# Layer A of a two-layer encoder trunk: two seven-product blocks for each pair of units, and their place in the second unit

## The chip, the cores and the metric

The kernel runs on one core of a Trainium2 chip. The metric is the device time of one execution in microseconds. A core has five engines that run side by side, each through its own instructions in a fixed order: TensorE (PE in the profile; PEld is its loading of the stationary operand), VectorE (DVE), ScalarE (ACT), GpSimd (POOL) and SyncE (SP). They wait for one another by semaphores. Transfers (DMA) are issued from the queues of SP, ACT and POOL. Matmuls write to eight banks of PSUM, a small memory from which DVE and ACT read the results.

## The reference

The input is one sequence of 256 frames of width 2048. There are two layers. Layer A (chunked attention with a relative bias) and layer B (attention with forget gates against shared keys and values) each have 32 heads of 128. What matters here is the first half of layer A:

```python
h = rms_norm(x, a_norm[layer])
q, k, v, g = jnp.split(h @ a_w_in[layer], 4, axis=-1)
o = chunked_relbias_attention(split_heads(q), split_heads(k), split_heads(v),
                              a_rel_bias[layer]).reshape(b, s, D_INNER)
x = x + (o * jax.nn.silu(g)) @ a_w_out[layer]
```

`a_w_in` is 2048 x 16384, `a_w_out` 4096 x 2048, all in float32.

## The kernel before

**Units and blocks.** All projections are cut into *units* of 512 output columns, 256 frames and the whole inner dimension. A unit accumulates in two PSUM banks, one for each half (`t`) of the frames. The inner dimension of layer A's input projection is 2048, that is 16 slices of 128; two slices (KB = 2) are a *block*, so a unit has eight blocks. A block's weights come in one load of 512 KB on SP's queue (`Feed.load`, line 208; six buffers, RAW).

**Splits.** Each float32 factor is split in a high and a low half in the format that TensorE takes at full rate. For a block of weights ACT rounds the high half (line 249 in `Feed.prepare`) and DVE subtracts to get the low half (line 250). A product is then three matmuls: high by high, high by low, low by high (`mm3`, line 178, for plain blocks; `dot3`, line 547, elsewhere). A plain block is 2 slices x 2 halves of the frames x 3 = 12 matmuls. The splits have four buffers each (SPLIT = 4) and are prepared three ahead of the block at which TensorE is (DEPTH = 3, `Feed.fill`). A buffer can be written again when TensorE has read what was in it.

**Groups, pairs and quads.** Two heads (HG = 2) are a group, and there are 16 groups. In layer A a group needs two units, which make a *pair*: one of queries and keys (`aqk`), one of values and gates (`avg`). Where the same block of both units is taken together, there are two slices of x by two halves of the frames on one side, and two slices of weights by two units on the other: a 2 x 2 by 2 x 2 product of tiles. Class `Quad` does it with seven products instead of eight, by the scheme of Strassen in Winograd's form: 21 matmuls instead of 24. It works in four parts (`Quad.split(i)`, i = 0 to 3, one split buffer each; the third is half as wide): the first unit's weights; the sums `t` of the two units' weights (lines 303 and 304); the second unit's second slice; and a last sum, formed in place by lines 312 and 313 on DVE. `Quad.step` (line 316) issues the matmuls, of which some go to the units' own accumulators and four (p1, p5, p7, p6) to four banks of their own. At the last quad of a run ACT and DVE (lines 352 to 356) combine these four into `comb`, which is added when the units are closed. The sums of x that a quad needs are formed once (`Quads.sum_up`, line 387).

Before the change, every pair of layer A from group 1 on has one quad, of block 7, behind the fifth of the seven plain blocks of its first unit (QUAD_STEP = 5). The 14 other blocks are plain.

**Attention beside the matmuls.** The attention of a group is a generator (`side_a`, line 711, and `attention`, line 552) whose steps are carried out between the blocks of the following units. `drive` (line 749) calls `advance` behind the blocks that a table names: `{3: 1}` means one step behind block 3. The steps in order: queries and keys from the accumulators (line 725) to `qk`; their transposition; their splits (`wide`, `q`, line 540 and 541); scores and softmax in two steps; the gates times the softmax's scale (`sg`) and their transposition; the split of the transposed weights; the second product; the output `oT` and its splits. In before, the queries and keys of a group are closed at the start of its second unit, and its attention runs from there into the next pair's second unit.

**Transposition.** `turn` (line 513) transposes 32 x 32 squares on DVE (line 518) and then moves them by 16 small transfers (line 521). In layer A twelve of the 16 of queries and keys are issued by POOL and four by ACT, and all 16 of `sg` by POOL. In layer B POOL and SP issue eight each.

Program order on an engine is the order in which the code issues, moved a little by the layer that builds the program. `issue_after` holds an instruction behind a named one, and `feed.behind` (line 264) is a tiny ACT operation that does the same through data.

## Time and profile before

| | us |
|---|---|
| median of 3 runs | 1731.91 (1731.39 to 1732.01) |
| the profiled execution | 1731.21 |
| its span, first to last instruction | 1729.5 |
| layer A's pairs of groups 1 to 14 (53.82 to 656.18) | 602.36, or 43.03 each |

In the profile a row of a timeline is: start, duration, engine, line, operation, output<-inputs, shape, and in brackets how long the engine had been idle and what ended it. Names of tiles lack their buffer numbers. `first` is the tile that holds the quads' sums `t` in one half and the transposed rows of queries and keys in the other; `sums` holds the sums of x in one half and the transposed queries and keys in the other. A row of windows gives the stretch, its length, and the busy time of each engine with the number of instructions.

### The profile page before, as it was taken

The numbers are of one execution on the slowest core, as the hardware profiler recorded it, in microseconds if no ns is written. First come the engines' busy times: TensorE is split into PE (matmuls) and PEld (weight loads), VectorE is DVE, ScalarE is ACT, GpSimd is POOL, SyncE is SP. The second block draws the span as 40 slices with busy tenths as digits, with TensorE's granted clock in tenths as the row PEclk, the third lists the DMA queues.
The fourth block names the chain that finished last, engine by engine and source line by source line (L and its number), as shares of the span: only waits on it lengthen the run. The fifth ranks groups of instructions, "written<-read, shape, count | busy, mean of one in ns | idle before, by whom it ended". The sixth has DMA issues, their size and how long they took to land.

```text
span 1729.5 us, 26618 instructions
## 1 busy us (share of the span) xinstructions
PE 1714.6 (99%) x8258; PEld 1505.1 (87%) x8258; DVE 1499.0 (87%) x2282; ACT 1186.5 (69%) x2163; POOL 394.7 (23%) x815
## 2 busy tenths in 40 slices
PE   9999999999999999999999999999999999999997
PEld 7888888888888888888888888888888888888886
DVE  7888888888888888888978999999999999996887
ACT  7666666666666666655658787788778887875554
POOL 2332333333333333212102222222222222221000
PEclk9999999999999999999999999999999999999999
DMA  8776777777777767576766666666666666767654
GB/s 307 243 230 226 232 231 230 228 229 229 229 228 226 233 224 233 190 260 216 264 214 222 219 238 230 225 230 231 227 228 233 231 227 228 261 228 247 219 195 146
DMA packets 147245, 396.41 MB, mean 229 GB/s; under 512 B 31104, under 2 KB 45728, under 8 KB 146976
## 3 DMA queue, kind: packets, MB, share of 16 engines
q1 hardware_dynamic: 119248, 363.71, 62.2%
q0 software_dynamic: 24064, 27.84, 5.4%
q10 hardware_dynamic: 3792, 3.17, 0.6%
q8 instruction: 66, 1.08, 0.3%
q14 instruction: 75, 0.61, 0.1%
HBM read 351.05 MB, written 4.23 MB: 205 GB/s over the span
## 4 chain that ended last, share of the span: by engine, by line
PE 96%; DVE 1%; DMA 1%; ACT 1%; issue 0%; SPq 0%; POOL 0%; ACTq 0%; DVEq 0%
PE bkv_acc L186 17%; PE avg_acc L186 17%; PE bqg_acc L186 17%; PE aqk_acc L186 16%; PE bo_acc L186 8%; PE ao_acc L186 7%; PE p L549 2%; PE p L548 2%; PE p L550 2%; PE op L612 1%; PE s0p L572 1%; DMA bo_raw<-in_b_w_out 0%; PE s1p L550 0%; PE s1p L549 0%; PE s1p L548 0%; PE op L550 0%
## 5 line engine op out<-in xcount | busy, mean ns | idle before, releaser
L521 POOL DMA_DIRECT2D sums<-first x320 | 157.3, 499 | 432.8 <-issue 157.8
L521 POOL DMA_DIRECT2D sgZ<-sgY x384 | 188.1, 497 | 154.5 <-DVE sgY L518 96.0
L244 ACT ACTIVATE bqg_hi<-bqg_raw,gain 128x512 fp32r<-128x512 f32 x226 | 150.0, 713 | 85.6 <-DMA bqg_raw<-in_b_w_in 27.4
L245 DVE SCALAR_TENSOR_TENSOR bkv_lo<-bkv_raw,gain,bkv_hi 128x512 fp32r<-128x512 f32 x226 | 162.0, 764 | 18.2 <-ACT bkv_hi L244 17.8
L186 PE MATMUL aqk_acc<-aqk_hi,xTh 128*128 128x512 f32 x452 | 167.5, 382 | 1.0 <-ACT aqk_hi L249 1.0
L249 ACT ACTIVATE avg_hi<-avg_raw 128x1024 fp32r<-128x1024 f32 x112 | 116.1, 1050 | 75.5 <-PE avg_acc L186 49.9
L186 PE MATMUL bkv_acc<-bkv_hi,x1Th 128*128 128x512 f32 x452 | 167.5, 382 | 0.0
L186 PE MATMUL bqg_acc<-bqg_hi,x1Th 128*128 128x512 f32 x452 | 167.4, 382 | 0.0
L186 PE MATMUL avg_acc<-avg_hi,xTh 128*128 128x512 f32 x452 | 167.4, 382 | 0.0
L186 PE MATMUL aqk_acc<-aqk_lo,xTh 128*128 128x512 f32 x452 | 166.3, 379 | 0.7 <-DVE aqk_lo L250 0.7
L186 PE MATMUL bqg_acc<-bqg_hi,x1Tl 128*128 128x512 f32 x452 | 166.1, 379 | 0.0
L186 PE MATMUL avg_acc<-avg_hi,xTl 128*128 128x512 f32 x452 | 166.1, 379 | 0.0
L186 PE MATMUL bqg_acc<-bqg_lo,x1Th 128*128 128x512 f32 x452 | 166.1, 379 | 0.0
L186 PE MATMUL bkv_acc<-bkv_hi,x1Tl 128*128 128x512 f32 x452 | 166.1, 379 | 0.0
L186 PE MATMUL bkv_acc<-bkv_lo,x1Th 128*128 128x512 f32 x452 | 166.1, 379 | 0.0
L186 PE MATMUL aqk_acc<-aqk_hi,xTl 128*128 128x512 f32 x452 | 166.1, 379 | 0.0
L186 PE MATMUL avg_acc<-avg_lo,xTh 128*128 128x512 f32 x452 | 166.1, 379 | 0.0
L250 DVE TENSOR_TENSOR avg_lo<-avg_raw,avg_hi 128x1024 fp32r<-128x1024 f32 x112 | 136.4, 1218 | 31.1 <-ACT avg_hi L249 31.1
L244 ACT ACTIVATE bkv_hi<-bkv_raw,gain 128x512 fp32r<-128x512 f32 x226 | 145.1, 711 | 23.2 <-issue 15.8
L245 DVE SCALAR_TENSOR_TENSOR bqg_lo<-bqg_raw,gain,bqg_hi 128x512 fp32r<-128x512 f32 x226 | 156.3, 742 | 4.8 <-ACT bqg_hi L244 4.8
L250 DVE TENSOR_TENSOR aqk_lo<-aqk_raw,aqk_hi 128x1024 fp32r<-128x1024 f32 x110 | 134.1, 1222 | 25.4 <-ACT aqk_hi L249 17.6
L249 ACT ACTIVATE aqk_hi<-aqk_raw 128x1024 fp32r<-128x1024 f32 x110 | 115.6, 1051 | 42.2 <-PE avg_acc L186 28.5
(379 smaller groups left out, 4332.9 us busy)
## 6 DMA issues: line engine op xcount, KB each, us to landing
bqg_raw<-in_b_w_in SPq DMA_DIRECT2D x128, 512.0 KB, 4.9
bkv_raw<-in_kv_w SPq DMA_DIRECT2D x128, 512.0 KB, 4.8
avg_raw<-in_a_w_in SPq DMA_DIRECT2D x127, 512.0 KB, 4.8
aqk_raw<-in_a_w_in SPq DMA_DIRECT2D x125, 512.0 KB, 4.6
ao_raw<-in_a_w_out SPq DMA_DIRECT2D x64, 512.0 KB, 4.5
bo_raw<-in_b_w_out SPq DMA_DIRECT2D x64, 512.0 KB, 4.4
sgZ<-sgY POOLq DMA_DIRECT2D x384, 40.0 KB, 2.9
sums<-first POOLq DMA_DIRECT2D x320, 32.0 KB, 3.4
```

Source lines behind the costliest of these rows:

```text
L186: pe.matmul(acc[t], x[:, t * P:(t + 1) * P], w, start=t not in begun, stop=last and i == 2)
L244: self.by_act = act.activation(hi[:, j], raw[:, j], AF.Copy, scale=gk)
L245: self.by_dve = dve.scalar_tensor_tensor(lo[:, j], raw[:, j], gk, r32(hi[:, j]), op0=OP.mult, op1=OP.subtract)
L249: self.by_act = act.activation(hi[:, j], raw[:, j], AF.Copy)
L250: self.by_dve = dve.tensor_sub(lo[:, j], raw[:, j], r32(hi[:, j]))
L521: queues[j].dma_start(out=r32(z)[j * SQ:(j + 1) * SQ, i], in_=y[i * SQ:(i + 1) * SQ, j])
L548: pe.matmul(out_, a[0], b[0], start=start, stop=False)
L549: pe.matmul(out_, a[0], b[1], start=False, stop=False)
L550: pe.matmul(out_, a[1], b[0], start=False, stop=stop)
L572: pe.matmul(s0p[:, i], q0[:, i], qkT[:, HG + i, 0], start=True, stop=True)
L612: pe.matmul(op[:, i, 1::NT], v1[:, i * DH:(i + 1) * DH], pT[:, i, NT], start=False, stop=i == HG - 1)
```

## The change

Every pair of layer A from group 1 on gets two quads, of blocks 6 and 7, and twelve plain blocks. They stand in the second unit, behind its plain blocks 1 and 2, so that one plain block lies between them. The first unit's six plain blocks all come before, and its accumulators are complete only at the end of the second quad. There `products` combines, closes queries and keys and issues two steps of the new group's attention (`advance(side, 2)`: `qk`, and its transposition). The remaining steps follow the tables A1_STEPS and A2_STEPS in the next pair. In group 0 the sums of x for both blocks are formed inside the second unit. The transfers of layer A's transpositions are issued by POOL and SP in turn (HALVES), as in layer B, and none by ACT. At the start of the output projection of layer A the last group's steps stand at other places. `feed.behind` in the quads' splits goes, and all quads are held by `issue_after`. Layer B is written differently in a few places but issues what it did.

```diff
-QUAD_STEP = 5
-QUAD_STEP_B = 3
-SECOND_STEPS = {0: 1, 6: 1}
-FIRST_STEPS = {0: 2, 2: 1}
-OLD_A_STEPS = {1: 1, 3: 99}
+QUADS_A = (1, 2)
+QUADS_B = (2,)
+A1_STEPS = {3: 1, 4: 2}
+A2_STEPS = {0: 1, 3: 1, 4: 99}
...
             if not i:
-                if not self.w:
-                    feed.behind(t[:, 0, :, :1], -1)
...
-                with tc.issue_after(feed.by_dve.ins) if self.w else nullcontext():
+                with tc.issue_after(feed.by_dve.ins):
                     dve.tensor_sub(t[:, 0], two[:, 0], one[:, 0])
                     dve.tensor_sub(t[:, 1], two[:, 1], two[:, 0])
...
-    def paired(specs, n):
-
-        quad = Quad(a_quads, specs, KD // KB - 1, True, True)
-        plain = whole(specs[0]) + whole(specs[1])
-        todo.extend(plain[:n] + [(None, quad)] + plain[n:])
-        return quad
-
-    a_pairs = [paired(qkvg[2 * g:2 * g + 2], QUAD_STEP) for g in range(1, NG)]
+    def paired(specs, places):
+
+        n = len(places)
+        quads = [Quad(a_quads, specs, KD // KB - n + i, not i, i == n - 1) for i in range(n)]
+        todo.extend(whole(specs[0]))
+        for i, item in enumerate(whole(specs[1])):
+            todo.append(item)
+            todo.extend((None, quads[k]) for k in range(n) if places[k] == i)
+        return quads
+
+    a_pairs = [paired(qkvg[2 * g:2 * g + 2], QUADS_A) for g in range(1, NG)]
...
+    HALVES = (pool, sp) * (NQ // 2)
...
-        yield from attention(g, biases, qk, vg, halfA, oA, (pool, pool, pool, act), (2, 2), home)
+        yield from attention(g, biases, qk, vg, halfA, oA, HALVES, ("last", "last"), home)
...
+    sums2 = big_tile([P, 2, 2, 4, P], F32R, name="sums2")
     rs, prev = [], None
     for g in range(NG):
         accs = {}
         if g:
             first, second = (Unit(xT, next(order)) for _ in range(2))
-
-            def products():
-                a_pairs[g - 1].step(xT, first, second)
-                for t in range(NT):
-                    act.activation(a_quads.comb[:, t], a_quads.comb[:, t], AF.Copy, scale=rsA[:, t:t + 1])
-
-            accs["qk"] = drive(rest(first), prev, FIRST_STEPS, {QUAD_STEP - 1: products})
-            vg = rest(second)
+            accs["qk"] = drive(rest(first), prev, A1_STEPS)
+            side = side_a(g, accs)
+
+            def products(quad):
+                quad.step(xT, first, second)
+                if quad.last:
+                    for t in range(NT):
+                        act.activation(a_quads.comb[:, t], a_quads.comb[:, t], AF.Copy, scale=rsA[:, t:t + 1])
+                    advance(side, 2)
+
+            hooks = {i: lambda quad=quad: products(quad) for i, quad in zip(QUADS_A, a_pairs[g - 1])}
+            accs["vg"] = list(drive(rest(second), prev, A2_STEPS, hooks))
         else:
             first, second = woven_units()
             rsA, halfA = rs
-            accs["qk"], vg = first.acc, rest(second)
-        old, prev = prev, side_a(g, accs)
-        advance(prev)
-        accs["vg"] = list(drive(vg, prev, SECOND_STEPS, {}, old, OLD_A_STEPS))
-        if not g:
-            a_quads.sum_up(xT, KD // KB - 1, sums[:, 0], a_quads.comb)
+            accs["qk"] = first.acc
+            side = side_a(g, accs)
+            advance(side)
+            sum_hooks = {1: lambda: advance(side)}
+            for i, b in ((2, KD // KB - 1), (4, KD // KB - 2)):
+                sum_hooks[i] = lambda b=b: a_quads.sum_up(xT, b, (sums if b % 2 else sums2)[:, 0], a_quads.comb)
+            accs["vg"] = list(drive(rest(second), None, {}, sum_hooks))
+        prev = side
         close_vg(accs, g)
...
-    project(oA, ao, ao_order, ao_begun, ao_closed, [(prev, [1, 0, 2, 6, 2, 1]), (ao_quads.open(oA, QUADS), [3, 1, 1, 2, 26])])
+    project(oA, ao, ao_order, ao_begun, ao_closed, [(prev, [4, 1, 0, 1, 4, 1, 1]), (ao_quads.open(oA, QUADS), [3, 1, 1, 2, 26])])
```

The built programs show where things stand. First DVE around the quad of a pair before the change (group 3); `sg`, `csc` and `sgY` belong to the attention of the group before:

```order
L250 TENSOR_TENSOR aqk_lo_1490<-aqk_raw_1317,aqk_hi_1489 128x1024
L303 TENSOR_TENSOR first_102<-avg_raw_1337,aqk_raw_1335 128x512
L594 RECIPROCAL csc<-sm 128x4
L595 TENSOR_TENSOR csc<-csc,half_a 128x4
L310 TENSOR_TENSOR quad_lo_1511<-aqk_raw_1335,quad_hi_1510 128x1024
L518 STREAM_TRANSPOSE sgY<-sg 128x1280
L312 TENSOR_TENSOR aqk_raw_1335<-avg_raw_1337,first_102 128x512
L310 TENSOR_TENSOR quad_lo_1555<-first_102,quad_hi_1554 128x1024
L313 TENSOR_TENSOR aqk_raw_1335<-aqk_raw_1335 128x512
L310 TENSOR_TENSOR quad_lo_1571<-avg_raw_1337,quad_hi_1570 128x512
L310 TENSOR_TENSOR quad_lo_1593<-aqk_raw_1335,quad_hi_1592 128x1024
L250 TENSOR_TENSOR aqk_lo_1605<-aqk_raw_1385,aqk_hi_1604 128x1024
```

The same engine in the changed program, from the last low half of the first quad of group 3 to that of the second:

```order
L306 TENSOR_TENSOR quad_lo_1659<-aqk_raw_1419,quad_hi_1658 128x1024
L249 TENSOR_TENSOR avg_lo_1671<-avg_raw_1472,avg_hi_1670 128x1024
L299 TENSOR_TENSOR first_102<-avg_raw_1492,aqk_raw_1490 128x512
L300 TENSOR_TENSOR first_102<-avg_raw_1492 128x512
L306 TENSOR_TENSOR quad_lo_1685<-aqk_raw_1490,quad_hi_1684 128x1024
L306 TENSOR_TENSOR quad_lo_1694<-first_102,quad_hi_1693 128x1024
L308 TENSOR_TENSOR aqk_raw_1490<-avg_raw_1492,first_102 128x512
L306 TENSOR_TENSOR quad_lo_1704<-avg_raw_1492,quad_hi_1703 128x512
L309 TENSOR_TENSOR aqk_raw_1490<-aqk_raw_1490 128x512
L306 TENSOR_TENSOR quad_lo_1722<-aqk_raw_1490,quad_hi_1721 128x1024
```

Before, plain blocks stood on both sides of the one quad; now the second quad's sums and splits stand behind a single plain low half (`avg_lo`). The same lines of code have lower numbers in the changed file: 249 is 250 of before, 299, 300, 308 and 309 are 303, 304, 312 and 313, and 306 is 310.

TensorE at the last part of such a second quad (group 4 of the changed program), with the plain block behind it:

```order
L551 MATMUL avg_acc_1887<-quad_hi_2140,sums 128x512
L549 MATMUL aqk_acc_1886<-quad_hi_2158,xTh_106 128x512
L549 MATMUL p_2094<-quad_hi_2158,sums 128x512
L550 MATMUL aqk_acc_1886<-quad_lo_2159,xTh_106 128x512
L551 MATMUL aqk_acc_1886<-quad_hi_2158,xTl_108 128x512
L550 MATMUL p_2094<-quad_lo_2159,sums 128x512
L551 MATMUL p_2094<-quad_hi_2158,sums 128x512
L185 MATMUL avg_acc_1887<-avg_hi_2170,xTh_105 128x512
```

In the code the three matmuls of each product stand together; in the built order both that need only the high half (`quad_hi`) stand ahead of the first that needs the low half (`quad_lo`). At the first quad of a pair, and everywhere before the change, they stand as in the code.

More of the change, by code (lines that the diff above doesn't have):

```diff
@@ L286, in __init__ @@
             self.all, self.specs, self.b, self.first, self.last = all_, specs, b, first, last
-            self.w = specs[0]["g0"] is not None or all_.w
         def split(self, i):
@@ L358, in trunk, with __init__ @@
     class Quads:
-        def __init__(self, name, w):
-            self.name, self.w, self.sums = name, w, {}
+        def __init__(self, name):
+            self.name, self.sums = name, {}
         def order(self, first, second, n, lead):
@@ L433, in trunk @@
     for g in range(NG):
-        qkvg.append(spec(f"bqg{g}", b_w_in[g], KD, g0=GB, quads=g > 0))
-        qkvg.append(spec(f"bkv{g}", kv_w[g], KD, g0=GKV, quads=g > 0))
+        qkvg.append(spec(f"bqg{g}", b_w_in[g], KD, g0=GB, quads=len(QUADS_B) * (g > 0)))
+        qkvg.append(spec(f"bkv{g}", kv_w[g], KD, g0=GKV, quads=len(QUADS_B) * (g > 0)))
     bo = [spec(f"bo{u}", b_w_out[u], KI, LATE if u == 3 else 0, KEPT if u == 3 else 0) for u in range(4)]
     todo += whole(qkvg[2 * NG]) + whole(qkvg[2 * NG + 1])
-    b_pairs = [paired(qkvg[2 * g:2 * g + 2], KD // KB - 1 + QUAD_STEP_B) for g in range(NG + 1, 2 * NG)]
+    b_pairs = [paired(qkvg[2 * g:2 * g + 2], QUADS_B) for g in range(NG + 1, 2 * NG)]
     bo_order = whole(bo[0]) + whole(bo[1])
@@ L550, in dot3, with attention @@
         pe.matmul(out_, a[1], b[0], start=False, stop=stop)
-    def attention(g, biases, qk, vg, half, ocat, queues, line, home, turned=(pool,) * NQ):
+    def attention(g, biases, qk, vg, half, ocat, queues, line, home):
         z = turn(qk.rearrange("p t (c d) -> p (t c) d", d=DH), NT * 2 * HG, "qk", queues, home)
@@ L600, in attention @@
                                scale=c[:, t, i:i + 1])
-        z = turn(sg, HG * NB + NT * HG, "sg", turned)
+        z = turn(sg, HG * NB + NT * HG, "sg", queues)
         pT = z[:, :, :HG * NB].rearrange("p i (h c) u -> p h c i u", h=HG)
@@ L951, in side_b @@
             evac_scaled(kv, 0, GC, rsB, qk[:, :, GC:])
-        rest_of = attention(g, biases, qk, lambda: (v, gs), halfB, oB, (pool, sp) * (NQ // 2), ("last", "last"), home, (pool, sp) * (NQ // 2))
+        rest_of = attention(g, biases, qk, lambda: (v, gs), halfB, oB, HALVES, ("last", "last"), home)
         next(rest_of)
@@ L972, in products @@
             def products():
-                b_pairs[g - 1].step(x1T, first, second)
+                b_pairs[g - 1][0].step(x1T, first, second)
                 open_b(accs, g)
@@ L977, in products @@
                     act.activation(k, k, AF.Copy, scale=rsB[:, t:t + 1])
-            accs["kv"] = drive(rest(second), prev, B2_STEPS, {QUAD_STEP_B - 1: products})
+            accs["kv"] = drive(rest(second), prev, B2_STEPS, {QUADS_B[0]: products})
         else:
```

8 lines of the change are left out of this document (4 added, 4 removed).

## The prediction

> **What bounds the kernel now.** I read the page's busy times first, then its chain, then the windows of single pairs of layer A and of layer B, and last the waits of TensorE.
>
> ```profile
> span 1729.5 us, 26618 instructions
> PE 1714.6 (99%) x8258; PEld 1505.1 (87%) x8258; DVE 1499.0 (87%) x2282; ACT 1186.5 (69%) x2163; POOL 394.7 (23%) x815
> PE 96%; DVE 1%; DMA 1%; ACT 1%; issue 0%; SPq 0%; POOL 0%; ACTq 0%; DVEq 0%
> 31.67:53.82 22.15, 22.15 (x108) 19.45 (x108) 14.84 (x23) 13.13 (x24) 8.00 (x14) 1.00 0.78 251
> 139.87:182.90 43.03, 43.03 (x210) 37.96 (x210) 36.70 (x52) 27.69 (x51) 13.91 (x29) 1.00 0.70 229
> 1045.06:1518.83 473.77, 473.60 (x2300) 417.51 (x2300) 435.99 (x738) 378.75 (x760) 99.36 (x199) 1.00 0.67 232
> PE ao_acc L549 <- DVE quad_lo L310: 1.0, 2, 0.7
> ```
>
> The windows give us, then busy PE, PEld, DVE, ACT and POOL, the granted clock (1.00), and DMA. A pair of layer A (139.87 to 182.90) takes 43.03 us and TensorE works through all of it, so only fewer matmuls can shorten it. DVE is busy for 36.70 of the 43.03. The last row counts: in the whole A projection TensorE waited 1.0 us for the low half of a quad. So far the quads cost TensorE next to nothing; the question is whether two in a row still do.
>
> **What is removed.** What a matmul costs is its distance from the next, not its duration.
>
> ```profile
> 150.07 0.38 PE L548 MATMUL p<-quad_hi,xTh 128*128 128x512 f32 x1
> 154.39 0.38 PE L550 MATMUL p<-quad_hi,sums 128*128 128x512 f32 x1
> ```
>
> These are the first and the last of a quad's 21 matmuls: 20 steps in 4.32 us, 0.216 us each, though each lasts 0.38. A plain pair of blocks is 24 matmuls, a quad 21, and 15 pairs get one quad more: 45 matmuls, 9.7 us, or 0.65 us a pair. That is all there is to gain: a pair could fall to 42.38 us.
>
> **What is added on DVE and ACT.** A quad needs its sums and four splits where two plain blocks need two splits.
>
> ```profile
> 143.50 0.68 DVE L303 TENSOR_TENSOR first<-avg_raw,aqk_raw 128x512 f32<-128x512 f32 x1
> 144.10 0.17 DVE L594 RECIPROCAL csc<-sm 128x4 f32<-128x4 f32 x1
> 147.60 0.65 DVE L312 TENSOR_TENSOR aqk_raw<-avg_raw,first 128x512 f32<-128x512 f32 x1
> 148.17 1.22 DVE L310 TENSOR_TENSOR quad_lo<-first,quad_hi 128x1024 fp32r<-128x1024 f32 x1
> 149.30 0.68 DVE L313 TENSOR_TENSOR aqk_raw<-aqk_raw 128x512 f32<-128x512 f32 x1
> 149.90 0.68 DVE L310 TENSOR_TENSOR quad_lo<-avg_raw,quad_hi 128x512 fp32r<-128x512 f32 x1
> 150.27 1.06 ACT L309 ACTIVATE quad_hi<-aqk_raw 128x1024 fp32r<-128x1024 f32 x1 [1.96 <-PE aqk_acc L186]
> 151.36 1.23 DVE L310 TENSOR_TENSOR quad_lo<-aqk_raw,quad_hi 128x1024 fp32r<-128x1024 f32 x1 [0.77 <-ACT quad_hi L309]
> 155.14 1.22 DVE L250 TENSOR_TENSOR avg_lo<-avg_raw,avg_hi 128x1024 fp32r<-128x1024 f32 x1
> 156.28 0.68 DVE L353 TENSOR_TENSOR comb<-comb,p 128x512 f32<-128x512 f32 x1
> ```
>
> From start to start, a wide DVE operation takes 1.13 us (148.17 to 149.30, or 155.14 to 156.28), a half one 0.60 (149.30 to 149.90), L312 0.57. A quad is 3 x 1.13 + 0.60 for the low halves and 3 x 0.60 + 0.57 for the sums, 6.4 us; two plain splits were 2.3. DVE gains 4.1 us a pair: 36.7 becomes 40.8, of 42.38. As a sum it fits, with 1.6 us to spare. (ACT gains 1.5 x 1.06 on 27.69, and has room.)
>
> **The critical place: from the first quad to the end of the second.** Four split buffers turn round. The plain block between the quads is split into the buffer of the first quad's first part, so its split starts when TensorE has read that part. Behind it DVE has, in the order shown above the prediction, the plain low half, two sums, two low halves, a sum, a half low half, the last sum; ACT must then split the last part, and DVE its low half. How such a hand-over runs, and what a late low half does, the A projection shows:
>
> ```profile
> 745.16 0.38 PE L550 MATMUL ao_acc<-quad_hi,oAl 128*128 128x512 f32 x1
> 745.63 1.06 ACT L249 ACTIVATE ao_hi<-ao_raw 128x1024 fp32r<-128x1024 f32 x1 [0.24 <-PE ao_acc L550]
> 818.28 1.23 DVE L310 TENSOR_TENSOR quad_lo<-ao_raw,quad_hi 128x1024 fp32r<-128x1024 f32 x1 [1.20 <-ACT quad_hi L309]
> 818.48 0.38 PE L548 MATMUL ao_acc<-quad_hi,oAh 128*128 128x512 f32 x1
> 819.56 0.48 PE L549 MATMUL ao_acc<-quad_lo,oAh 128*128 128x512 f32 x1 [0.70 <-DVE quad_lo L310]
> 819.88 0.38 PE L550 MATMUL ao_acc<-quad_hi,oAl 128*128 128x512 f32 x1
> ```
>
> The part was read at 745.16 + 0.38 = 745.54 and ACT began 0.09 later (0.04 behind some others in layer A; I take 0.065). ACT to DVE is 0.03: 150.27 + 1.06 = 151.33, and 151.36. The late low half ended at 819.51; the matmul behind it counts from 819.66 (0.48 is 0.10 more than the usual 0.38), 0.15 later.
>
> Now the walk, from the end of the last matmul of the first quad's first part as 0. ACT splits the plain block from 0.07 to 1.13; DVE has its low half from 1.16, L299 from 2.29, L300 from 2.89 (done 3.58), the second quad's first low half from 3.49. ACT splits the sums from 3.61 to 4.65, so the next low half starts at 4.68 (DVE would be free at 4.62), L308 at 5.81, the half low half at 6.39, L309 at 6.99, done 7.67. ACT splits the last part from 7.70 to 8.76; its low half runs from 8.79 to 10.01, and the matmul counts from 10.16.
>
> TensorE wants it earlier. The reference point is the end of a matmul that started 0.38 before. Between it and the last part stand 42 matmuls: 6 + 3 + 6 of the first quad, 12 of the plain block, 6 + 6 + 3 of the second quad. The last part's first two need only the high half (the built order puts both ahead), so the 45th needs the low half: -0.38 + 45 x 0.216 = 9.34. It waits **0.82 us**, in each of 15 pairs, where 0.65 us was saved.
>
> What speaks for more: if DVE comes more than 0.2 us late to the block between the quads, all of that lateness is added. For less: hand-overs at the shortest seen (0.04, and 0.05 into TensorE's weight load) make it 0.70. I keep 0.82, nearest to the rows that show both ends; the bounds are 0.70 and, with DVE 1 us late, 1.8.
>
> **The rest.** (a) Half of the transposition transfers go from POOL to SP, and the four that ACT issued go to SP too. The trace of before shows that form only in layer B:
>
> ```profile
> 164.53 1.23 DVE L518 STREAM_TRANSPOSE first<-qk 128x1024 f32<-128x1024 f32 x1
> 178.53 0.42 ACT L540 ACTIVATE wide<-sums 128x256 fp32r<-128x256 f32 x1
> 1082.95 1.24 DVE L518 STREAM_TRANSPOSE first<-qk 128x1024 f32<-128x1024 f32 x1
> 1084.26 6.21 SPq L521 DMA_DIRECT2D sums<-first  x8
> 1084.73 3.93 POOL L521 DMA_DIRECT2D sums<-first  x8 [13.45 <-PE bqg_acc L186]
> sums<-first POOLq DMA_DIRECT2D x320, 32.0 KB, 3.4
> sums<-first SPq DMA_DIRECT2D x128, 32.0 KB, 2.1
> aqk_raw<-in_a_w_in SPq DMA_DIRECT2D x125, 512.0 KB, 4.6
> ```
>
> There the transposition ends at 1084.19, SP's last transfer is out at 1090.47 and lands 2.1 later, 8.4 us behind it; POOL's land by 1092.1. In layer A today 12.8 us pass between the end at 165.76 and the use at 178.53. Continuing the walk (21 us of DVE work behind the last low half, of which 11 stand ahead of the transposition) the use comes some 8 us behind it: about even, with another 0.8 us until lateness would reach the block between the quads. Behind SP's waiting transfers stand loads of weights; a load lands in 4.6 us, and the first that is queued there, the first quad's own weights, is wanted some 5 us after SP is free. Layer B queues the same way and loses 0.17 us in 473.77 (the window above). I take nothing; the bounds are 0 and 1 us a pair, the late-transfer rival.
>
> [...]
>
> (b) Group 0 forms the sums of one more block, and both inside its second unit: an added 3 us of DVE (one 0.68, four small, two low) where DVE has 22.15 - 14.84 = 7.3 us idle. Nothing; at most 1 us, once. (c) At the start of the A projection four more splits of the last group fall in a crowded stretch: 0 to 1 us, once. I take 0.3 for (b) and (c) together. (d) The small ACT operations that held back the splits go; ACT is not late anywhere, so nothing. (e) The attention's steps stand at other blocks of the pair, with the same instructions on DVE, ACT and TensorE and the same transfers; on DVE they are counted in the walk, and the scores' matmuls find queries and keys split some 1.5 us before their turn, unless the transfers are late.
>
> The sum, against the profiled execution's own 1731.21 us (1.7 us around its span of 1729.5): 1731.2 - 9.7 + 15 x 0.82 + 0.3 = 1734.1. The median of the three runs, 1731.91, is 0.7 above that execution, so **1734.8 us** is expected as the median: 0.17% above before.
>
> **Rivals.** *The wait stays away* (1722.2 to 1728): the last low half is in time or nearly so, and the full 9.7 us is kept, 1731.9 - 9.7 = 1722.2. For it: DVE has 1.6 us to spare as a sum, and layer B runs with DVE at 92% (435.99 of 473.77) without a stall. Against it: layer B has one quad a pair, and the walk is not a matter of load but of one chain of 10.2 us against 9.7 us of matmuls, in which every link has a row.
>
> *The transfers are late* (1742 to 1752): the transposed queries and keys land after ACT wants them, ACT stands with the next block's split behind them, and DVE enters the first quad late. It decides once the transfers take over about 9 us from the transposition's end: then each further microsecond is added in full to 0.82, 15 us over the layer at 1 us. For it: POOL's gaps between issues, and less than 1 us of slack. Against it: 8.4 us in layer B. This is the one that ends clearly slower: 1734.8 + 15 x 0.5 to 15 x 1.1.
>
> *DVE's pitch is longer.* A held start would make each of the chain's seven DVE links 0.09 longer, 0.6 us a pair, 1744. The rows speak against it: 155.14 + 1.22 = 156.36, and the next began at 156.28. [...]
>
> *The change does nothing to the layer* (1731 to 1733): wait and saving cancel, 0.65 each. It lies inside the uncertainty of the walk.
>
> **How the numbers follow.** The walk holds (0.6 to 1.05 us of wait): 0.58, 1731.3 to 1738; a little over half of it lies within 0.2% (3.5 us, about what a measurement of this kernel can tell from no change). The wait stays away: 0.15. The transfers or the pitch: 0.22, 1740 to 1752. Anything else: 0.05. Faster by over 0.2% (below 1728.4): 0.16; within: 0.43; slower (above 1735.4): 0.41. The range from 1726 to 1745 leaves out most of the first rival and the far end of the second; the likeliest case alone is 1731 to 1738.
>
> **What would show it.** In the windows of after, a pair should take about 43.2 us with TensorE busy for 42.4, and the idle time should be one piece of 0.8 us ahead of a matmul of line 550 (of the changed kernel) that reads the fourth low half of the second quad. DVE should show about 40.8 us busy, with two pauses of about 1 us, ahead of the last low half of each quad. No wait in the first quad; the transposed queries and keys used within 0.5 us of landing. If the pair takes 42.4 and no such wait stands in the table, the walk is wrong, most likely in the order of the low halves. If waits stand at the block between the quads or in the first quad, DVE came late and the transfers are to blame.

## The result and the profile after

The changed kernel takes 1757.51 us (median of 4, 1755.68 to 1759.02) where the kernel before took 1731.96 beside it: a ratio of 1.0146, with a 95% interval of 1.0128 to 1.0163. It is 1.5% slower. The forecast was 1734.8, within 1726 to 1745. The page of the profiled execution first, span, busy times and chain:

```profile
span 1754.5 us, 27007 instructions
...
PE 1721.5 (98%) x8213; PEld 1499.6 (85%) x8213; DVE 1560.7 (89%) x2378; ACT 1200.3 (68%) x2115; POOL 300.7 (17%) x623
...
PE 84%; DVE 6%; DMA 5%; issue 2%; ACT 2%; SPq 0%; ACTq 0%; POOL 0%; DVEq 0%
```

The span is 25.0 us longer than before. TensorE's share of the chain falls from 96% to 84%: 6% of the chain is now DVE, 5% transfers, and 2% "issue", time in which an engine waits for nothing that the profile names. The waits of TensorE in the table of waits (us in all, times, longest):

```profile
PE aqk_acc L550 <- DVE quad_lo L306: 8.4, 15, 0.6
PE op L549 <- ACT wide L541: 2.6, 1, 2.6
PE op L613 <- DMA avg_raw<-in_a_w_in: 2.5, 7, 0.4
PE op L613 <- issue: 1.4, 4, 0.4
...
PE op L613 <- DMA aqk_raw<-in_a_w_in: 1.1, 3, 0.4
```

The first row is the wait that was forecast: 15 times, once a pair, ahead of the fourth low half of the second quad. The other rows were not forecast. The second is a single wait in the output projection. The three of line 613 stand ahead of the four matmuls that read the transposed probabilities themselves. The windows (us, then busy PE, PEld, DVE, ACT, POOL, the granted clock, DMA) show a usual pair, a long one, and the output projection of layer A:

```profile
127.52:171.62 44.10, 43.19 (x207) 37.24 (x207) 40.87 (x58) 28.88 (x48) 8.02 (x17) 1.00 0.66 224
470.00:516.00 46.00, 44.13 (x207) 37.53 (x206) 39.42 (x56) 28.68 (x48) 7.83 (x17) 1.00 0.64 214
714.60:885.29 170.69, 166.40 (x765) 144.52 (x764) 150.74 (x208) 97.91 (x143) 27.65 (x58) 0.99 0.69 232
```

In the profile of before the projection was this row:

```profile
695.34:860.89 165.55, 164.04 (x766) 142.44 (x764) 148.09 (x204) 96.24 (x141) 27.86 (x58) 1.00 0.70 233
```

A usual pair takes 44.10 us, not 43.2, and the projection costs 5.1 more. Of these, 2.6 us are the single wait for the last group's split probabilities (750.62). As it ended, TensorE's granted clock fell to 0.50 for 3.41 us, which stretched the matmuls there by another 1.6. One more is lost at the last group's scores, behind a stop of POOL of 1.86 us (from 716.72 in the trace; run 11 is about these stops). The clock in the windows:

```profile
750.44:753.85 3.41, 3.23 (x13) 3.05 (x14) 2.66 (x5) 1.06 (x3) 0.80 (x3) 0.50 0.90 356
```

**Inside the second quad.** The timeline of one pair, DVE and ACT from the block between the quads on, TensorE at both ends of the two quads:

```profile
115.75 0.38 PE L549 MATMUL p<-quad_hi,xTh 128*128 128x512 f32 x1
...
116.83 0.38 PE L551 MATMUL aqk_acc<-quad_hi,xTl 128*128 128x512 f32 x1
...
118.39 1.23 DVE L249 TENSOR_TENSOR avg_lo<-avg_raw,avg_hi 128x1024 fp32r<-128x1024 f32 x1
...
120.13 0.69 DVE L300 TENSOR_TENSOR first<-avg_raw 128x512 f32<-128x512 f32 x1
...
120.93 1.06 ACT L305 ACTIVATE quad_hi<-first 128x1024 fp32r<-128x1024 f32 x1 [1.33 <-DVE first L300]
...
124.37 0.69 DVE L309 TENSOR_TENSOR aqk_raw<-aqk_raw 128x512 f32<-128x512 f32 x1
...
125.15 1.06 ACT L305 ACTIVATE quad_hi<-aqk_raw 128x1024 fp32r<-128x1024 f32 x1 [0.83 <-DVE aqk_raw L309]
...
125.90 0.38 PE L551 MATMUL avg_acc<-quad_hi,sums 128*128 128x512 f32 x1
...
126.24 1.23 DVE L306 TENSOR_TENSOR quad_lo<-aqk_raw,quad_hi 128x1024 fp32r<-128x1024 f32 x1 [1.18 <-ACT quad_hi L305]
126.26 0.48 PE L549 MATMUL aqk_acc<-quad_hi,xTh 128*128 128x512 f32 x1
126.58 0.38 PE L549 MATMUL p<-quad_hi,sums 128*128 128x512 f32 x1
...
127.52 0.48 PE L550 MATMUL aqk_acc<-quad_lo,xTh 128*128 128x512 f32 x1 [0.56 <-DVE quad_lo L306]
127.84 0.38 PE L551 MATMUL aqk_acc<-quad_hi,xTl 128*128 128x512 f32 x1
...
128.27 0.38 PE L551 MATMUL p<-quad_hi,sums 128*128 128x512 f32 x1
```

From the first matmul of the first quad (115.75) to the last of the second (128.27) are 53 steps, 11.45 us at 0.216 each; it took 12.52, so **1.07 us** are lost here. The rows say where: the low half's matmul comes 0.72 late (127.52 - 126.58 - 0.216) and the step behind it is 0.10 longer, together 0.82. That this is the forecast's own number is luck: the high half is late as well, by 0.14 (126.26 - 125.90 - 0.216) and again 0.10 behind it, and the low half itself is later than the walk has it. The walk's zero is 116.83 + 0.38 = 117.21; there the low half counts from 10.16, here from 127.84 - 0.216 = 127.62, which is 10.41. Of these 0.25 us, 0.14 are the hand-overs from DVE to ACT, which the walk put at 0.03 each: they took 0.11 (120.82 to 120.93) and 0.09 (125.06 to 125.15). The rest is hundredths in many links, 0.02 of it a slip in the sum (3.61 + 1.06 is 4.67, not 4.65).

**At the op matmuls.** TensorE at the products with the values, and DVE at the low half of their split (L542), in the timeline:

```profile
266.02 0.27 PE L549 MATMUL op<-wide,vh 128*128 128x256 f32 x1
...
267.27 0.76 DVE L542 TENSOR_TENSOR wide<-sgZ,wide 128x256 fp32r<-128x256 f32 x2
...
267.74 0.19 PEld L550 LDWEIGHTS op<-wide,vh 128*128 128x128 f32 x1
267.86 0.27 PE L550 MATMUL op<-wide,vh 128*128 128x256 f32 x1
...
268.30 0.28 PE L551 MATMUL op<-wide,vl 128*128 128x256 f32 x1
268.93 0.68 PE L613 MATMUL op<-sgZ,v 128*128 128x128 f32 x4 [0.35 <-DMA avg_raw<-in_a_w_in]
269.37 0.46 PE L185 MATMUL avg_acc<-avg_hi,xTl 128*128 128x512 f32 x1
```

The weight load at 267.74 comes right behind the first of DVE's two low halves (267.69 in the trace): here TensorE's queue stands. A matmul of 256 columns takes 0.11, so 268.93 is 0.52 late; the four take 0.44 against 0.37 where nothing holds them (180.34 to 180.71 in run 2): **0.60 us a pair**. The releaser that the profile names, a load of weights, has nothing to do with these operands. What TensorE's queue did meanwhile stands in the table of line 613 (instructions, ns at least, in the median and at most, first and last start):

```profile
L613 PEldq EVENT_SEMAPHORE  x256: 51/51/51, 91.7 to 1625.3; - x128
```

It checked semaphores, 256 instructions of 51 ns for the 32 groups of both layers, 8 for each. Their price is more than their duration: in the trace of this group the eight start 0.106 us apart on average (268.08 to 268.82). Eight checks were not new either. In before the table counts four for each group of layer A and eight for each of layer B:

```profile
L612 PEldq EVENT_SEMAPHORE  x192: 51/51/51, 81.5 to 1599.8; - x192
```

Yet 15 of layer B's 16 groups lose nothing at them. There the split's low half ends 0.3 to 4.6 us before the first op matmul, and the last check starts 0.17 to 2.5 us ahead of the four matmuls behind it (2.9 in layer A's pairs); in the one group that loses, 0.34, the low half ends 0.07 behind the start of the first op matmul, and the last check starts 0.11 ahead of the four, as in all 15 pairs of the changed kernel.

| term, us over the layer | forecast | measured |
|---|---|---|
| 45 matmuls saved | -9.7 | -9.7 |
| wait at the second quad, 15 pairs | +12.3 (0.82 each) | +16.0 (1.07 each) |
| op matmuls, 15 pairs | 0 | +9.0 (0.60 each) |
| four pairs longer than 44.10 (44.70, 44.54, 46.00, 44.45) | 0 | +3.3 |
| output projection, 170.69 against 165.55 | +0.3, with group 0 | +5.1 |
| not placed | | +1.3 |
| span | +2.9 | +25.0 |

The expectations below put 0.85 at the second quad and 0.25 at the scores. The finer reading here came later: 1.07 at the quads, and the 0.25 was the mean over ten pairs of 0.6 and 1.9 us in two of them.

### The profile page after: what moved, and what is told of

Read it like the earlier page. It is cut to its first block, busy times and chain, and to the rows that moved or that the text cites. A ratio compares the mean times of both kernels' runs of the same rounds, so it can differ in the third digit from the quotient of the medians.

```text
span 1754.5 us, 27007 instructions
## 1 busy us (share of the span) xinstructions
PE 1721.5 (98%) x8213; PEld 1499.6 (85%) x8213; DVE 1560.7 (89%) x2378; ACT 1200.3 (68%) x2115; POOL 300.7 (17%) x623
## 3 DMA queue, kind: packets, MB, share of 16 engines
q10 hardware_dynamic: 720, 1.07, 0.2%
## 4 chain that ended last, share of the span: by engine, by line
PE 84%; DVE 6%; DMA 5%; issue 2%; ACT 2%; SPq 0%; ACTq 0%; POOL 0%; DVEq 0%
PE bkv_acc L185 17%; PE bqg_acc L185 17%; PE aqk_acc L185 13%; PE avg_acc L185 9%; PE bo_acc L185 8%; PE ao_acc L185 6%; PE p L550 2%; PE p L551 2%; PE p L549 2%; DVE avg_lo L249 2%; DMA aqk_raw<-in_a_w_in 2%; DMA avg_raw<-in_a_w_in 1%; ACT quad_hi L305 1%; PE op L613 1%; DVE quad_lo L306 1%
## 5 line engine op out<-in xcount | busy, mean ns | idle before, releaser
L522 POOL DMA_DIRECT2D sums<-first x256 | 125.8, 499 | 563.0 <-ACT aqk_hi L248 254.4
L522 POOL DMA_DIRECT2D sgZ<-sgY x256 | 125.5, 498 | 155.1 <-PE avg_acc L185 80.1
L185 PE MATMUL aqk_acc<-aqk_hi,xTh 128*128 128x512 f32 x392 | 145.7, 385 | 0.0
L185 PE MATMUL avg_acc<-avg_hi,xTl 128*128 128x512 f32 x392 | 144.8, 383 | 0.0
L185 PE MATMUL aqk_acc<-aqk_lo,xTh 128*128 128x512 f32 x392 | 143.7, 380 | 1.0 <-DVE aqk_lo L249 1.0
L185 PE MATMUL avg_acc<-avg_lo,xTh 128*128 128x512 f32 x392 | 144.4, 382 | 0.0
L185 PE MATMUL aqk_acc<-aqk_hi,xTl 128*128 128x512 f32 x392 | 143.7, 380 | 0.0
L185 PE MATMUL avg_acc<-avg_hi,xTh 128*128 128x512 f32 x392 | 143.7, 380 | 0.0
L249 DVE TENSOR_TENSOR avg_lo<-avg_raw,avg_hi 128x1024 fp32r<-128x1024 f32 x97 | 115.9, 1222 | 11.7 <-ACT avg_hi L248 10.8
L249 DVE TENSOR_TENSOR aqk_lo<-aqk_raw,aqk_hi 128x1024 fp32r<-128x1024 f32 x95 | 114.5, 1218 | 5.3 <-ACT aqk_hi L248 5.3
```

Source lines behind the costliest of these rows:

```text
L185: pe.matmul(acc[t], x[:, t * P:(t + 1) * P], w, start=t not in begun, stop=last and i == 2)
L249: self.by_dve = dve.tensor_sub(lo[:, j], raw[:, j], r32(hi[:, j]))
L522: queues[j].dma_start(out=r32(z)[j * SQ:(j + 1) * SQ, i], in_=y[i * SQ:(i + 1) * SQ, j])
```

## The experiments

Times are medians, each compared with the kernel before on the same chip. Where a kernel has the sums first, its lines from 307 on are one higher than in the changed kernel.

**1. The transfers undone.**

```diff
-    yield from attention(g, biases, qk, vg, halfA, oA, HALVES, ("last", "last"), home)
+    yield from attention(g, biases, qk, vg, halfA, oA, (pool, pool, pool, act), ("last", "last"), home, (pool,) * NQ)
```

> Undoes the transfers alone, in layer A: the queries and keys by POOL three times and ACT, the probabilities by POOL, as before; quads and steps as in the changed kernel. In the changed kernel a pair takes 44.10 us against the 42.38 that the saved matmuls would leave; 0.85 of the 1.72 lie at the second quad, 0.60 at the four op matmuls that read the transposed probabilities themselves, 0.25 at the scores. Theory 'number of semaphores': those matmuls wait for 16 transfers, checked by 8 instructions of 51 ns each on TensorE's queue where before had 4, so with POOL alone at the probabilities the 0.60 falls by 4 x 0.051 = 0.2 or more, and the 0.25 by 0.1: 0.3 a pair, some 5 us in all, about 1752. Theory 'no lead' (TensorE's queue has just stood at a late split, so any check is seen): the op matmuls still lose over 0.3, and the rest is as in the other theory or less. Rival 'late transfers': POOL alone is slower, waits for DMA appear ahead of the splits, 1757 or more. The 0.85 at the second quad stays in all.

1771.54 us, 1.0222 (1.0205 to 1.0239): slower still, so the rival holds for the time. The checks at the op matmuls went as expected, in the table of that line 4 for each of layer A's 16 groups and 8 for layer B's:

```profile
L613 PEldq EVENT_SEMAPHORE  x192: 51/51/51, 91.6 to 1642.9; - x192
```

The loss there fell from 0.60 to 0.17. That is more than four times 51 ns, and just four times the 0.106 us from check to check. But queries and keys came late, up to 2.4 us, in the table of waits:

```profile
PE s1p L549 <- ACT q L541: 4.9, 5, 2.4
```

With the closing where it now stands, the old issuers cost 14 us more than half by SP.

**2. Products and scores a block later behind their splits.**

```diff
-A1_STEPS = {3: 1, 4: 2}
-A2_STEPS = {0: 1, 3: 1, 4: 99}
+A1_STEPS = {3: 1, 5: 2}
+A2_STEPS = {0: 1, 3: 1, 5: 99}
```

> Transfers as in the changed kernel (16 waited for, by two issuers), but in layer A the products with the values come one block later behind their split, and the scores one block later behind theirs. Theory 'no lead': with the splits done well ahead, TensorE's queue runs ahead of the array again and the 8 checks vanish behind running matmuls: 0.60 falls to 0.15 or less, 0.25 to 0.15 or less; some 0.5 a pair, 15 x 0.5 = 8 us, 1749 to 1750. Theory 'number of semaphores': 8 checks of 51 ns cost the same wherever they stand, 1757. The 0.85 at the second quad stays in both.

1754.34 us, 1.0129 (1.0113 to 1.0144), where 1749 to 1750 was expected. The loss at the op matmuls is gone, with 8 checks as in the changed kernel; the timeline:

```profile
180.23 0.28 PE L551 MATMUL op<-wide,vl 128*128 128x256 f32 x1
180.34 0.61 PE L613 MATMUL op<-sgZ,v 128*128 128x128 f32 x4
180.71 0.72 PE L185 MATMUL aqk_acc<-aqk_hi,xTh 128*128 128x512 f32 x2
```

0.11 from the first row to the second, nothing lost. So the eight checks, 0.52 in the changed kernel, cost nothing where the queue has a lead. A pair fell to 43.76, by 0.34 and not 0.60, since a row of the waits has grown:

```profile
PE aqk_acc L549 <- ACT quad_hi L305: 4.4, 16, 0.7
```

The two quads now take 12.72, 0.2 more. TensorE reaches them earlier; DVE, which now has the later softmax just ahead of them, does not (in run 8, which leaves the softmax where it was, nothing comes back).

**3. The two quads apart**, with the steps of attention one block later.

```diff
-QUADS_A = (1, 2)
-A1_STEPS = {3: 1, 4: 2}
-A2_STEPS = {0: 1, 3: 1, 4: 99}
+QUADS_A = (1, 3)
+A1_STEPS = {4: 1, 5: 2}
+A2_STEPS = {0: 1, 4: 1, 5: 99}
```

> Both quads stay, but two plain blocks stand between them instead of one (behind the second and the fourth block of the second unit), and the attention's steps move one block back with them. Walk: between the end of the first quad's first part and the last low half TensorE has 12 more matmuls, 2.6 us, while DVE and ACT have one more split, 1.1: the last low half is in time by about 0.6, the 0.85 a pair at the second quad goes, 15 x 0.85 = 12.7, about 1745. Rival 'DVE has too much to do': the wait only moves to another block, 1754 to 1758. The losses at the op matmuls and the scores stay (0.85 a pair), since their steps keep their distances.

1767.58 us, 1.0207 (1.0192 to 1.0223): the walk's expectation of 1745 failed, and the rival's 1754 to 1758 too. Two waits from the table:

```profile
PE aqk_acc L185 <- DVE qk L726: 7.3, 14, 0.5
PE aqk_acc L550 <- DVE quad_lo L306: 3.6, 16, 1.2
```

The wait at the quads shrank but did not go (65 steps, 14.04 us, took 14.85), and a new one stands at the start of the next pair: its first unit needs the accumulator that DVE empties (L726) only behind the later closing. The place of the closing binds the place of the quads; distance alone is no cure.

**4. One quad a pair, all else as changed.**

```diff
-QUADS_A = (1, 2)
+QUADS_A = (2,)
```

> One quad a pair as before, at the second quad's place in the second unit; transfers, closing and steps as in the changed kernel. Walk: no second quad, no wait (0.85 gone), 45 plain matmuls more (9.7): 1757.5 + 9.7 - 12.8 = 1754.4, and a pair of 43.03 + 0.85 = 43.9 with all of its excess at the op matmuls and the scores. Rival 'the place is to blame' (the quad in the second unit, next to the close, is late even alone): the wait ahead of the quad's low half stays at 0.3 or more a pair, 1759 to 1767.

1746.64 us, 1.0087 (1.0072 to 1.0102). The pair is as expected, with no wait at the quad:

```profile
140.00:183.91 43.91, 43.53 (x211) 37.99 (x210) 36.89 (x52) 26.88 (x46) 8.02 (x17) 1.00 0.69 224
```

43.91 is 43.03 plus 0.88 at the op matmuls. My sum of 1754.4 for the whole was wrong beside it: it took 0.85 for the 1.07 at the second quad, and the long pairs and the projection as unchanged, while they shrank too. So with nothing of the second quad in it the change still loses 15 us: **most of the slowdown is not the quads.**

**5. Another order of the second quad's sums on DVE.**

```diff
-            feed.by_dve = dve.tensor_sub(lo[:, :n], src, r32(hi[:, :n]))
+            with tc.issue_after(self.summed.ins) if i == 1 else nullcontext():
+                feed.by_dve = dve.tensor_sub(lo[:, :n], src, r32(hi[:, :n]))
...
-                dve.tensor_sub(one[:, 1], one[:, 1], one[:, 0])
+                self.summed = dve.tensor_sub(one[:, 1], one[:, 1], one[:, 0])
```

> The changed kernel with one order altered on DVE in the second quad: the two sums of its last part stand ahead of the second part's low half instead of on both sides of the half low half. Walk: ACT can split the last part when the plain block's buffer is read, near 5.95 instead of 7.70, and the last low half ends near 8.8 instead of 10.0, in time for 9.34; the second part's low half ends near 7.1 and is wanted at 7.2, so up to 0.1 of wait appears there. Of the 0.85 a pair some 0.75 goes: pairs of about 43.35, 15 x 0.75 = 11 us, about 1746. Rival 'DVE comes late to the whole place': the lateness shows at the second part's low half instead, over 0.5 a pair, and the time falls by 4 us or less, 1753 to 1757. Op matmuls and scores keep their losses.

1750.68 us, 1.0111 (1.0096 to 1.0126). TensorE at the second part of the second quad:

```profile
123.59 0.38 PE L550 MATMUL p<-quad_hi,sums 128*128 128x512 f32 x1
124.01 0.48 PE L551 MATMUL p<-quad_lo,sums 128*128 128x512 f32 x1
124.33 0.38 PE L552 MATMUL p<-quad_hi,sums 128*128 128x512 f32 x1
```

The wait of the last part is gone, and the one that the walk put in its place, at the second part's low half, is there: 0.20 and 0.10, where "up to 0.1" was expected. The two quads take 11.75 instead of 12.52, 0.77 less for an expected 0.75. The walk gives the right places; its sizes are off by a tenth or two. The time fell by 6.8 and not 11 us, mainly because the op matmuls gave back 0.5: TensorE, no longer held at the quads, now comes ahead of the split's low half, and the loss there is 1.09.

**6. Both, and the last group's split later.** Edits 2 and 5, and in the projection:

```diff
-[(prev, [4, 1, 0, 1, 4, 1, 1])
+[(prev, [4, 1, 0, 1, 5, 1, 1])
```

> Three edits in one: products and scores a block later behind their splits (the earlier run that did this alone took 3.2 us off, with its pair at 43.76 and all of the rest, 1.27 a pair, at the second quad), the order of the sums as in the run beside this one, and in the output projection of layer A the last group's split of the probabilities one block later. If the walk's order is what holds the second quad, 1.27 falls to 0.5 or less there (0.1 and the 0.4 by which DVE came late in the earlier run), the pair to 43.0 or less, and with 2.6 us less of waiting at the projection's start the time is 1754.3 - 15 x 0.77 - 2.6 = about 1740. If DVE's lateness is what is left, the pair stays at 43.5 or more: 1748 or more.

1745.37 us, 1.0084 (1.0069 to 1.0099). About 1740 was expected. A usual pair is 42.95, for the first time below before's 43.03, but two take 47.38 and 46.37. The third edit did not help: the projection took 173.45, with one wait of 5.5 us at the last group's first op matmul.

**7. The transfers alone, in the kernel before.**

```diff
-(pool, pool, pool, act), (2, 2), home)
+(pool, sp) * 2, (2, 2), home, (pool, sp) * 2)
```

> The kernel before with the transfers of layer A as in the changed kernel, half by POOL and half by SP, and nothing else: 16 transfers to wait for at the op matmuls, 8 checks instead of 4. Theory 'number of semaphores': 0.2 to 0.5 us a pair lost there, 15 pairs, 1735 to 1739. Theory 'no lead': the op product stands here in one piece well behind its split, TensorE's queue runs ahead and hides all 8 checks: 1731 to 1733, no loss at these matmuls beyond the 0.15 that before shows behind them.

1738.96 us, 1.0045 (1.0029 to 1.0062). The time is within the first theory's range, but not by its cause: the op matmuls lose nothing with 8 checks (0.12 from the last of the split's to the first of the four, 430.14 to 430.26; they stand two blocks behind their split in before), so "no lead" is right about the place, and over 7 us are lost elsewhere. Four of the fourteen pairs stay at 43.03; nine are 0.1 to 0.8 longer and one takes 44.84, the largest losses at the scores. One cause shows in the table of waits, here of this kernel:

```profile
DVE first L304 <- DMA avg_raw<-in_a_w_in: 28.2, 14, 3.8
```

In before the same row is 9.3 us, 13 times, at most 2.4: a quad's weights now wait in SP's queue behind the transfers. Most of it has cover; in the longest case DVE's splits for the scores came late. The rest, some 4 us of it in layer B, where no edit was made, is not traced.

**8. Edit 5, and only the op product a block later**; in the projection the quads, the split and the product later.

```diff
-A2_STEPS = {0: 1, 3: 1, 4: 99}
+A2_STEPS = {0: 1, 3: 1, 5: 99}
-ao_quads.order(ao[0], ao[1], 3, 13)
+ao_quads.order(ao[0], ao[1], 3, 16)
-[(prev, [4, 1, 0, 1, 4, 1, 1])
+[(prev, [4, 1, 0, 1, 6, 2, 1])
```

> On top of the run with the sums first (1750.7, pairs of 43.79): only the product with the values a block later behind its split (the scores stay where the changed kernel has them), and in the output projection of layer A the first quad three blocks later with the last group's split of the probabilities two and its product three blocks later. 'No lead': the wait for the late low half (0.4), the 8 checks (0.55) and their restarts (0.3) all go at the op matmuls, some 1.1 a pair, of which up to 0.3 comes back at the second quad because TensorE arrives there earlier: pairs of 42.7 to 43.0, 12 to 16 us; the 4.4 us at the projection's start go too, 4 us: 1731 to 1735. If the checks cost the same wherever they stand, the pair stays at 43.4 or more and the time at 1741 or more. The two pairs in which POOL pauses in its transfers stay 1 to 3 us longer than the others.

1742.75 us, 1.0059 (1.0045 to 1.0072), where 1731 to 1735 was expected. The pair, in the windows:

```profile
125.00:167.69 42.69, 42.65 (x208) 37.31 (x207) 40.78 (x58) 28.53 (x48) 8.04 (x17) 1.00 0.68 237
```

42.69 is the forecast's 42.38 plus the 0.30 left at the second quad. Nothing came back at the quads, since the softmax stayed where it was. All that remains lies in the long pairs (45.28, 43.10, 43.82, 43.13) and in the projection, 174.89 us.

**9. The probabilities by SP alone**, in the changed kernel.

```diff
-    z = turn(sg, HG * NB + NT * HG, "sg", queues)
+    z = turn(sg, HG * NB + NT * HG, "sg", turned or queues)
```

(`turned` is `(sp,) * NQ` in layer A.)

> The changed kernel with the transfers of the probabilities all by SP, those of queries and keys half by POOL as before: POOL has 8 transfers a pair instead of 16, and the op matmuls wait for 8 semaphores by 4 checks instead of 8. 'Pauses': in the traces so far POOL stops for 1.7 us after every 78 to 80 of its transfers, so in layer A it should stop once or twice (every tenth pair) instead of three times, and only those pairs be longer than 44.1 minus the saving. 'Lead and checks': with 4 checks the 0.60 at the op matmuls falls to 0.2 or less as in the run with POOL alone, 0.4 a pair, 6 us: 1749 to 1751. Rival 'late weights': 16 transfers in a row hold SP's queue for 10 us, loads of weights come late, waits for DMA of 1 us or more a pair appear: 1760 or more.

1799.39 us, 1.0388 (1.0370 to 1.0407): the rival. Loads of weights came late behind the long row of transfers on SP's queue; ACT, which splits the weights, waited 42.9 us for one unit's loads alone (in the changed kernel the table has no such row), and TensorE 24.4 us for the probabilities' split, which comes behind them on ACT and DVE:

```profile
ACT avg_hi L248 <- DMA avg_raw<-in_a_w_in: 42.9, 29, 3.5
PE op L550 <- DVE wide L542: 24.4, 15, 2.1
```

The probabilities themselves were there in time: in a usual pair they landed 6 to 8 us ahead of their split. With four checks the op matmuls lost 0.17, as in run 1. What it was also run for, it shows: POOL stopped once in layer A, at 525 us, and for the second time at 924.

**10. The last pair without quads**, its queries and keys closed behind the first unit, the projection in its old order, and edit 5 and the later op product kept.

```diff
-quads=len(QUADS_A) * (g > 0)
+quads=len(QUADS_A) * (0 < g < NG - 1)
...
+        if g == NG - 1:
+            first, second = (Unit(xT, next(order)) for _ in range(2))
+            accs["qk"] = drive(rest(first), prev, {3: 1, 4: 2, 6: 1})
+            side = side_a(g, accs)
+            advance(side)
+            hooks = {i: lambda n=n: advance(side, n) for i, n in ((0, 1), (4, 1), (6, 2))}
+            accs["vg"] = list(drive(rest(second), prev, {2: 1, 4: 99}, hooks))
...
-[(prev, [4, 1, 0, 1, 6, 2, 1])
+[(prev, [1, 5, 2, 1])
```

> The run with the product a block later (1742.75), with two changes at the end of layer A: the last group's pair has no quads (8 plain blocks a unit, 6 matmuls more, 1.3 us), so that its queries and keys close behind the first unit as in before, and the output projection has its old order with the last group's remaining steps early. Theory 'the end of layer A': the projection took 174.9 us there, 170.9 in the changed kernel and 165.6 before, because the last group's attention starts half a unit later and its product or its output is waited for; here it should take 166 to 168: 1742.75 + 1.3 - 7 to 9 = 1735 to 1737. If the projection stays at 170 or more, the late closing is not what costs there. Pairs of 42.69, and longer ones where POOL pauses, stay.

1729.87 us, 0.9991 (0.9982 to 1.0001): as fast as before, 13 us less than run 8 (1735 to 1737 was expected). The projection in the windows:

```profile
696.45:859.33 162.88, 162.39 (x755) 141.44 (x754) 144.81 (x194) 95.30 (x134) 23.89 (x50) 1.00 0.71 237
```

162.88, shorter even than before's 165.55, though in part because some of its matmuls (755 against 766) now stand in the pair ahead. The last pair and the projection together take 207.75 us, 217.57 in run 8 and 208.58 in before: the loss at the end of layer A is gone. The edit changes the closing and the projection's order at once, so which of the two does how much is not shown.

**11. The same, with group 0's queries and keys by POOL alone.**

```diff
-HALVES, ("last", "last"), home)
+HALVES if g else (pool,) * NQ, ("last", "last"), home, HALVES)
```

> The same, but group 0's queries and keys are transposed with all 16 transfers by POOL: 8 POOL transfers more ahead of the pairs, nothing else changed. 'Pauses': POOL stops for 1.7 us after every 78 to 80 of its transfers, so its stops now come 8 transfers earlier, in the transfers of the probabilities, which have 10 us of room, instead of those of queries and keys, which have 1; the pairs of 45.28, 43.10, 43.82 and 43.13 fall to about 42.7 and 4 to 5 us go: 1730 to 1733, as fast as before or faster. If the long pairs have another cause they stay where they are, and the time equals that of the run beside this one within 1.5 us.

1727.06 us, 0.9966 (0.9953 to 0.9979), 2.8 us less than run 10 for an expected 4 to 5. One of POOL's stops in the timeline of run 10, then of run 11:

```profile
266.92 2.46 POOL L523 DMA_DIRECT2D sums<-first  x5 [18.08 <-DVE oT L618]
271.02 1.49 POOL L523 DMA_DIRECT2D sums<-first  x3 [1.64 <-issue]
```

```profile
243.19 2.46 POOL L523 DMA_DIRECT2D sgZ<-sgY  x5 [6.67 <-DVE sgY L520]
247.33 1.49 POOL L523 DMA_DIRECT2D sgZ<-sgY  x3 [1.68 <-issue]
```

Eight more transfers in group 0 moved the stop out of the queries and keys (`sums`) into the probabilities (`sgZ`). With a stop the transfers come late by more than its own length, which is 1.65 us (from 274.39) and 1.76 (from 494.95) in two pairs of the changed kernel. There a usual pair's last transfer of queries and keys lands 1.0 to 1.7 us before its use; in the two with a stop the last one also lands 4.4 and 5.5 us after its issue, where 1.8 is usual, and ACT stands at the split:

```profile
281.94 0.42 ACT L541 ACTIVATE wide<-sums 128x256 fp32r<-128x256 f32 x1 [2.55 <-DMA avg_raw<-in_a_w_in]
```

The releaser named, a load of weights, is again not an operand; the last transfer landed at 281.41. The pairs of run 11 in one window:

```profile
64.89:650.00 585.11, 584.43 (x2822) 511.11 (x2822) 559.05 (x778) 390.41 (x643) 108.74 (x230) 1.00 0.68 230
```

Every long pair is gone: they take between 42.68 and 42.77 all along, and TensorE is busy for 584.43 of 585.11 us. The stop's place is the cause of the long pairs, and this kernel, 0.34% faster than before, beats both before and the change.

## Why the prediction was wrong

The forecast was a loss of 0.17%, within what a measurement can tell from no change; it is 1.5%, and the time lies 12.5 us above the range. Step by step:

- **What bounds the kernel, and the matmuls saved.** Right. Run 11's pair of 42.69 is 43.03 - 0.65 + 0.31, with two quads.
- **DVE's added work.** Right: 40.87 us a pair for a forecast 40.8, with a pause of about 1.1 us ahead of the last low half of each quad.
- **The walk.** The mechanism is right, and run 5, which altered one link, moved the wait to the place that the walk gives. The term was 0.82 and measures 1.07, 3.7 us more over the layer; the largest part of the difference is the hand-over from DVE to ACT, taken as 0.03 from one row of ACT to DVE.
- **(e), the attention's steps "stand at other blocks, with the same instructions".** This is the step that failed first. The products with the values stood two blocks behind their split before, and one block behind it now. Counted were the instructions, not the distance. With one block TensorE's queue stands at the late low half, loses its lead (the last check starts 0.11 us ahead of its matmul, 2.9 before), and the checks of semaphores behind it are no longer hidden: 0.60 us a pair, 9 us, the largest term that the forecast lacks. Where TensorE itself also waits for the low half, it is 0.88 and 1.09 (runs 4 and 5). Moving the product one block further takes it away (runs 2 and 8).
- **(a), half of the transfers by SP: "nothing".** Failed too, by three effects that I had no row for or dismissed: 8 checks instead of 4 at the op matmuls (0.60 against 0.17, run 1); weights queued behind the transfers (seen in run 7, which lost 7.6 us by the transfers alone, not all of it traced); and a margin of 1.0 to 1.7 us between landing and use, which POOL's stops, 1.65 and 1.76 us in the two pairs, and the late landings with them overrun. The prediction named "POOL's gaps between issues" under the late transfers, and gave that rival its condition, but not the stops in the trace of before, where 12.8 us passed between the transposition and the use and no pair was longer for them. Layer B, its model, issues the same way and hides the eight checks, since its splits end before the products need them (by 0.3 to 4.6 us in 15 groups of before).
- **(c), the start of the projection, 0 to 1 us once.** 5.1 us. I counted four more splits in a crowded stretch; what counts is that the last group's chain of scores, softmax, transfers and products starts half a unit later, and the projection waits for its end: 2.6 us at the products, 1.6 behind them at a granted clock of 0.50, and 1.0 at the scores. With the last pair closed early and the old order the loss is gone (run 10).
- **(b) and (d)** gave no wait that the profile shows.
- **The rivals.** "The wait stays away" is out, and so is "the change does nothing to the layer". "DVE's pitch is longer" is out too: from 118.39 to 120.13 a wide and a half operation took 1.74 us, and the walk has 1.13 + 0.60. "The transfers are late" came true in the pairs with a stop, not in all.

## What to carry to other kernels

When a step is moved, count the distance to what it waits for, in instructions of the waiting engine, as well as its instructions: here the product one block behind its operand's split lost 0.60 us a pair, most of it at checks that were hidden at two blocks. Look for rare stops (here POOL's, of 1.4 to 1.9 us and once 3.68, 78 transfers apart) in the stretches where they cost nothing today, and ask whether the change takes away their cover. Look at the end of the pipeline apart: here it paid once, 5.1 us, for the last group's later start, and the old schedule for that group alone took the loss away.

## What the runs showed of the hardware

- POOL stopped behind its 85th transfer and behind each 78th from there, whatever lay between them, in the four traces in which its transfers are counted here: nine times in before (1.40 to 1.87 us, once 3.68, from 516.38), and seven times each in the changed kernel (1.58 to 1.88), run 10 (1.56 to 1.88) and run 11 (1.42 to 1.88). With 8 transfers more in group 0 (run 11) the first stop came 8 transfers earlier in the order of the pairs, at 245.65 instead of 269.38. Why it stops is not shown.
- Each of the 256 instructions that check semaphores at the op matmuls took 51 ns, and the eight ahead of 268.93 started 0.106 us apart. In before, where the last check started 0.17 us or more ahead of its matmul, nothing was lost (31 of 32 groups); at 0.11 the matmul was 0.52 us late in the 15 pairs of the changed kernel and 0.34 in one group of before. Eight checks cost nothing in run 2 and in run 7 (0.11 and 0.12 from matmul to matmul); four made the next matmul 0.10 late in run 1. How far TensorE's queue can be ahead is not shown.
- Behind these stops of TensorE the next step was 0.10 us longer for matmuls of 512 columns (126.26 to 126.58, 127.52 to 127.84: 0.32 for 0.216), and 0.07 for the four at 268.93.
- At the end of the wait of 2.6 us in the projection the granted clock fell to 0.50 for 3.41 us, and a matmul of 256 columns took 0.21 us instead of 0.11 (751.85 to 752.06).
- In the split format a matmul of 512 columns takes 0.216 us from start to start and lasts 0.38, as the shortest of the nine in bfloat16 at the start of before. Two products of 128 columns left in float32 took four matmuls and 0.36 us in that trace (182.29 to 182.65), 0.18 each; 128 columns at the pace of the split ones are 0.054.
